# A feed-forward that makes the blocks' sums in steps: full rows of h issued with the norm

## The chip, the cores and the metric

One core of one Trainium2 chip runs the whole program as one launch. The metric is the device time of the launch in microseconds, as a median of several runs. The engines named here are PE (TensorE, matmuls), VectorE (DVE), ScalarE (ACT), and SyncE (SP), whose queue issues the loads.

## The reference, cut to what matters

The program is one inference step of a two-layer backbone on 640 tokens (512 latent, 128 context), width 1024, all in float32. Each layer is feed-forward, mixer, feed-forward. The feed-forward, and the modulation that it needs:

```python
def ffn_sub(x, g, shift, scale, gate, w_in, w_out):
    h = modulate(rms_norm(x, g), shift, scale)      # h * (1 + scale) + shift
    a, b = jnp.split(h @ w_in, 2, axis=-1)          # w_in: 1024 x 2*2816
    return x + gate * (FFN_RESIDUAL * ((jax.nn.silu(a) * b) @ w_out))

sh1, sc1, g1, sh2, sc2, g2, sh3, sc3, g3 = ada(cvec, p['w_mod'][l], p['b_mod'][l])
```

`ada` is silu(c) times a 1024 x 9216 matrix for each layer, for the latent and for the context condition.

## The kernel before

Activations lie transposed: eight tiles of 128 features by 640 tokens, split in two groups g of 320 columns. Float32 products are made from a hi and a lo half of each operand: for each weight tile ScalarE copies the hi half (L103, `whi`) and VectorE subtracts to the lo half (L104, `wlo`), and PE runs three matmuls (hi x hi, hi x lo, lo x hi; `mm3`, L132 to L135). A *unit* is one load of 128 x 1024 weights, that is one tile of 128 hidden features for a or for b: eight steps k of six matmuls for both groups, 48 matmuls. Written (2, a) here is the a-unit of hidden tile 2, counted from 0.

Of the 22 hidden tiles of each feed-forward the first `nconv` (5 in the first feed-forward, 4 in the others) are made with such units. All later ones are made by `product_set` with a scheme of Winograd's kind: seven products instead of eight on quarters of h and of the weights, 84 matmuls for an a- and a b-unit together. That scheme needs sums and differences of the four blocks h11, h12, h21, h22 of the full h (each 128 x 4 x 320, `hf`), and their hi and lo parts T1 to T4 (`Th`, `Tl`). `combine_h` makes them: first *full rows* (`h_full`, L398 on VectorE and L400 on ScalarE, one per feature tile and group), then the sums L443, L447, L448, L452 and the parts L430, L431; T4 (L436, L437) overwrites the split h after its last use. Group 1 of the full rows is made with the norm in the later feed-forwards (`apply_full`), group 0 in `combine_h`.

A later feed-forward starts with `start4`: four units, (0, a) to (1, b), are run for group 0 and then for group 1, since the norm of group 1 (`self.pend`) comes later. The first one starts with three units in `start_first`. Then `in_one` runs the units one by one, and `hidden` (L512 Silu, L516 product, L522 and L523 halves of hid) follows each pair.

Modulation: `mod_tile` loads 128 rows of w_mod (512 KB, `rawm`) and VectorE makes one sum for each condition (L157, two per tile; `sil` holds silu(c), loaded and made at L149 and L150). These tiles are fillers, given out by `filler` beside the units, product sets (`fill_set`) and output steps. They share a pool of four buffers with the weight loads (`raw`), while the split weights have five buffers (`wr`). SP issues loads in the program's order, and a load waits until its buffer is free.

In the feed-forwards the order on each engine comes from the tile scheduler, which starts from the program's order; in the mixers PE's order is written by hand. The order that was built stands further below where it matters.

Of the kernel before, what the change touches and what calls it, by code (L numbers as in the profile page):

```python
# [40 lines left out]
class Body:  # L41
# [311 lines left out]

    def start4(self, srcs, mid=None, late=None, between=None):

# [7 lines left out]
        def part(g, us):  # L363
            for u in us:
                p4[u][g] = self.bank()
            for k in range(KT):
                for u in us:
                    self.mm3([p4[u][g][:, :G]], w[u], k, [self.h(k, g)], k == 0, k == KT - 1)
                if (g, us[0], k) == (1, 1, 1) and late:
                    late()  # L370
                if (g, us[0], k) == (0, 2, 1) and self.pend:
                    self.pend()
                    self.pend = None
                    if mid:
                        self.lnexp()

        part(0, (0, 1))
# [36 lines left out]

    def combine_h(self, pool, l, s, all_groups):

        nc = self.nc
        (h11, h12), (h21, h22) = self.hf
        T = self.T = [None] * 4

        def full(r, gs):
            for k in range(4):
                for g in gs:
                    self.h_full(self.hf[r][g][:, k], 4 * r + k, g, l, s)

# [13 lines left out]
        if all_groups:  # L439
            full(0, (0, 1))  # L440
        else:
            full(0, (0,))
        nc.vector.tensor_tensor(h11, h12, h11, op=ALU.subtract)  # L443
        parts(0, h11)
        if all_groups:
            full(1, (1,))
        nc.vector.tensor_tensor(h12, h22, h12, op=ALU.subtract)  # L447
        nc.vector.tensor_tensor(h22, h22, h11, op=ALU.subtract)  # L448
        parts(1, h22)
        parts(2, h12)  # L450
        full(1, (0,))
        nc.vector.tensor_tensor(h21, h21, h22, op=ALU.subtract)  # L452
        return lambda: parts(3, h21)

# [39 lines left out]
    def ffn(self, ctx, l, j, nxt, fill=(), first=False):  # L494
# [3 lines left out]
        nconv = NCONV[2 * l + j]  # L498
        early = 8 - 4 * (nconv - 3) if first else 4
        spread = max(0, len(fill) - (32 if first else 28))  # L500
# [46 lines left out]

        def in_one(f, ab):
            w, p = self.unit(win[l, j, f, ab]), [self.bank() for _ in range(2)]
            for k in range(KT):  # L550
# [3 lines left out]
        if first:  # L554
            hid = [hidden(p3[0], p3[1])]
            hid.append(hidden(p3[2], in_one(1, 1)))
        else:
            self.h_blocks(hp)
            p4 = self.start4([win[l, j, f, ab] for f in range(2) for ab in range(2)])
            hid = [hidden(p4[0], p4[1]), hidden(p4[2], p4[3])]  # L560
        if fill:
            self.mod_load()
        if first:
            self.h_blocks(hp)
        while len(hid) < nconv:
            if len(hid) == 2:
                over = self.combine_h(Tp, l, 2 * j, first)
                self.hf = None
            pa = in_one(len(hid), 0)
            hid.append(hidden(pa, in_one(len(hid), 1)))  # L570
            if first and len(hid) > 3:
                filler(4)
        over()

# [791 lines left out]
def body(nc, tc, i, o):  # L1366
    with ExitStack() as ctx:
# [8 lines left out]
        with ExitStack() as c:  # L1376
            b.mod_begin(c)
            b.ffn(c, 0, 1, (1, 0), vf(0, range(2, 9))[52:] + vf(1, range(0, 3)))
        with ExitStack() as c:
            b.mod_begin(c)  # L1380
            b.ffn(c, 1, 0, (1, 1), vf(1, range(3, 9))[:44])
        with ExitStack() as c:
            b.mixer1(c, (1, 2))
        with ExitStack() as c:
            b.mod_begin(c)
            b.ffn(c, 1, 1, None, vf(1, range(3, 9))[44:])
        b.mm_close()
# [129 lines left out]
```

## Time and profile before

| | us |
|---|---|
| median of 3 runs | 2377.46 (2376.36 to 2379.68) |
| profiled execution | 2375.22 |
| its span | 2373.4 |
| PE busy | 2297.9 |
| VectorE busy | 1900.9 |
| ScalarE busy | 1124.8 |

The span is what the trace covers; the rest of the profiled execution lies around it. Busy times are sums over one engine's instructions. PE's is the largest by far, but matmuls are pipelined, so a busy PE need not be at full pace: the count of matmuls in a window tells its pace better.

### The profile page before, as it was taken

To read this page: it belongs to the slowest core of one execution; us is meant where nothing else is said; L and a number is where in the kernel's file an instruction comes from. 1 tells how busy PE (TensorE), PEld (TensorE's weight loads), DVE (VectorE), ACT (ScalarE), POOL (GpSimd) and SP (SyncE) were. 2 spreads that over 40 slices of the span, in tenths; PEclk is the share of its full clock that TensorE was granted. 3 is DMA by queue.
4 is the path that set the end of the run, shared out by engine and by line. 5 is a ranking of instruction groups with operands and counts; after the bars stand their busy time and mean duration, and the time that the engine had idled before them with its cause. 6 is when DMAs were issued, how large, how long until landed. Compare 5 with 4: busy or idle time off the path is not lost.

```text
span 2373.4 us, 40480 instructions
## 1 busy us (share of the span) xinstructions
PE 2297.9 (97%) x15912; PEld 2227.2 (94%) x15912; DVE 1900.9 (80%) x3779; ACT 1124.8 (47%) x2074; POOL 2.2 (0%) x10
## 2 busy tenths in 40 slices
PE   7899999999998999999999999998999999999998
PEld 4899999998888999999999999998888899999997
DVE  6998989785888978786789898969778888565665
ACT  5434343462666434334552525347756664253442
POOL 0000000000000000000000000000000000000000
PEclk9999999999999999999999999999999999999999
DMA  7354535332111434252225354432010013222221
GB/s 289 118 169 133 176 121 181 121 96 85 59 47 36 159 125 132 100 169 75 86 81 186 121 173 136 156 100 82 29 36 28 28 54 111 85 83 79 89 71 64
DMA packets 81086, 253.37 MB, mean 107 GB/s; under 512 B 9600, under 2 KB 15360, under 8 KB 80896
## 3 DMA queue, kind: packets, MB, share of 16 engines
q1 hardware_dynamic: 80896, 250.79, 32.3%
q8 instruction: 125, 2.05, 0.3%
q14 instruction: 65, 0.53, 0.1%
HBM read 247.34 MB, written 3.41 MB: 106 GB/s over the span
## 4 chain that ended last, share of the span: by engine, by line
PE 87%; DVE 9%; ACT 3%; issue 1%; DMA 1%; DVEq 0%; SPq 0%; ACTq 0%
PE mm L124 34%; PE mm L135 15%; PE mm L132 15%; PE mm L133 14%; PE tr L660 2%; PE pv L1293 2%; PE sc L1258 1%; DVE wlo L104 1%; DVE junk L157 1%; PE pv L1060 1%; ACT whi L103 0%; DVE Tl L431 0%; PE mm L810 0%; PE mm L809 0%; PE mm L808 0%
## 5 line engine op out<-in xcount | busy, mean ns | idle before, releaser
L103 ACT ACTIVATE whi<-raw 128x1024 fp32r<-128x1024 f32 (+2 forms) x419 | 406.9, 977 | 576.1 <-PE mm L133 281.1
L104 DVE TENSOR_TENSOR wlo<-raw,whi 128x1024 fp32r<-128x1024 f32 (+2 forms) x419 | 466.0, 1117 | 134.6 <-ACT whi L103 134.2
L132 PE MATMUL mm<-hid,whi 128*128 128x320 f32 x1408 | 427.1, 310 | 0.0
L133 PE MATMUL mm<-hid,whi 128*128 128x320 f32 x1408 | 425.7, 308 | 0.0
L124 PE MATMUL mm<-hhi,wlo 128*128 128x320 f32 x1136 | 351.5, 309 | 0.4 <-DVE wlo L104 0.4
L124 PE MATMUL mm<-hhi,whi 128*128 128x320 f32 x1136 | 351.3, 309 | 0.0
L124 PE MATMUL mm<-hlo,whi 128*128 128x320 f32 x1136 | 350.8, 309 | 0.0
L135 PE MATMUL mm<-hid,wlo 128*128 128x320 f32 x1408 | 346.1, 308 | 0.0
L157 DVE CUSTOM_DVE_ANT_0 junk<-rawm,sil 128x1024 bf16<-128x1024 f32 x256 | 312.0, 1219 | 16.4 <-DMA rawm<-in_wmT 14.4
L351 DVE SCALAR_TENSOR_TENSOR x<-mm,mod,x 128x192 f32<-128x192 f32 (+2 forms) x576 | 226.5, 433 | 116.8 <-PE mm L135 116.1
L132 PE MATMUL mm<-hhi,whi 128*128 128x320 f32 x896 | 280.3, 325 | 9.5 <-ACT hhi L298 6.8
L133 PE MATMUL mm<-hlo,whi 128*128 128x320 f32 x896 | 279.8, 318 | 0.5 <-DVE hlo L299 0.3
L133 PEld LDWEIGHTS mm<-hid,whi 128*128 128x128 f32 x1408 | 264.3, 188 | 0.8
L132 PEld LDWEIGHTS mm<-hid,whi 128*128 128x128 f32 x1408 | 264.3, 188 | 0.8
L135 PE MATMUL mm<-hhi,wlo 128*128 128x320 f32 x896 | 251.9, 316 | 12.9 <-DVE wlo L104 12.7
L135 PEld LDWEIGHTS mm<-hid,wlo 128*128 128x128 f32 x1408 | 241.6, 188 | 0.0
L124 PEld LDWEIGHTS mm<-hhi,wlo 128*128 128x128 f32 x1136 | 213.6, 188 | 0.8 <-DVE wlo L104 0.8
L124 PEld LDWEIGHTS mm<-hlo,whi 128*128 128x128 f32 x1136 | 213.7, 188 | 0.0
L124 PEld LDWEIGHTS mm<-hhi,whi 128*128 128x128 f32 x1136 | 213.7, 188 | 0.0
L132 PEld LDWEIGHTS mm<-hhi,whi 128*128 128x128 f32 x896 | 170.8, 193 | 19.7 <-ACT hhi L298 10.0
L135 PEld LDWEIGHTS mm<-hhi,wlo 128*128 128x128 f32 x896 | 165.1, 193 | 15.8 <-DVE wlo L104 14.9
L133 PEld LDWEIGHTS mm<-hlo,whi 128*128 128x128 f32 x896 | 173.3, 194 | 4.9 <-DVE hlo L299 2.6
(214 smaller groups left out, 4107.7 us busy)
## 6 DMA issues: line engine op xcount, KB each, us to landing
raw<-in_w_in SPq DMA_DIRECT2D x176, 512.0 KB, 3.6
rawm<-in_wmT SPq DMA_DIRECT2D x128, 512.0 KB, 3.6
raw<-in_w_out SPq DMA_DIRECT2D x64, 384.0 KB, 3.6
raw<-in_w_out SPq DMA_DIRECT2D x64, 320.0 KB, 3.0
wm<-in_wm SPq DMA_DIRECT2D x16, 512.0 KB, 10.2
raw<-in_w_ab SPq DMA_DIRECT2D x12, 512.0 KB, 4.1
raw<-in_w_c SPq DMA_DIRECT2D x10, 512.0 KB, 3.5
sil<-in_c SPq DMA_DIRECT2D x8, 512.0 KB, 5.5
```

Source lines behind the costliest of these rows:

```text
L103: a = (nc.scalar.activation(hi[:, :n], r[:, :n], AF.Copy), nc.vector.tensor_tensor(lo[:, :n], r[:, :n], hi[:, :n].bitcast(F32), op=ALU.sub ...
L104: nc.vector.tensor_tensor(lo[:, :n], r[:, :n], hi[:, :n].bitcast(F32), op=ALU.subtract))
L124: nc.tensor.matmul(out, a[:, c], b, start=start and first, stop=last, skip_group_check=True)
L132: nc.tensor.matmul(out, hi[:, c], rh, start=start, stop=False)
L133: nc.tensor.matmul(out, hi[:, c], rl, start=False, stop=False)
L135: nc.tensor.matmul(out, lo[:, c], rh, start=False, stop=stop)
L157: nc.vector.tensor_tensor_reduce(out=self.junk, in0=r, in1=self.sil[:, q], op0=ALU.mult, op1=ALU.add, scale=1.0, scalar=0.0, accum_out=sel ...
L351: nc.vector.scalar_tensor_tensor(out=x[:, c], in0=ps[:, c], scalar=self.mod[:, q, l, v, m:m + 1], in1=x[:, c], op0=ALU.mult, op1=ALU.add)
L660: self.nc.tensor.transpose(ps[:, a * P:(a + 1) * P], src[:, b * P:(b + 1) * P], self.ident)
L1060: nc.tensor.matmul(st["pv"][64 * f:64 * f + 64, ti * P:(ti + 1) * P], V[:, sl, vc[f]], st[ti, f][:, a * P:(a + 1) * P], start=a == 0, stop ...
L1258: nc.tensor.matmul(s[:, half], qs[e][:, ti * P:(ti + 1) * P], kd[kv][:, hl, half * G:half * G + G], start=hl == 0, stop=hl == 1)
L1293: nc.tensor.matmul(st["pv"][64 * f:64 * f + 64, ti * P:(ti + 1) * P], V[:, (4, 0, 1, 2, 3)[a], vc], rhs, start=a == 0, stop=a == 4)
```

## The change

The full rows of group 0 are issued in `start4`, right behind the norm of group 1, in the three later feed-forwards. `combine_h` becomes a generator: each step of it (a sum and its parts, or a set of full rows in the first feed-forward) is taken after the split of one unit of `in_one`, and what is left follows the last unit. The first feed-forward gives out its fillers singly, one per unit from hidden tile 3 on, four in all, and four in the first two product sets, where it gave out four behind each of hidden tiles 3 and 4. Eight modulation tiles move from the third feed-forward to the second.

```diff
--- before.py
+++ after.py
@@ -351,7 +351,7 @@
             nc.vector.scalar_tensor_tensor(out=x[:, c], in0=ps[:, c], scalar=self.mod[:, q, l, v, m:m + 1],
                                            in1=x[:, c], op0=ALU.mult, op1=ALU.add)
 
-    def start4(self, srcs, mid=None, late=None, between=None):
+    def start4(self, srcs, mid=None, late=None, between=None, hf=None):
 
         w = [self.unit(s) for s in srcs[:2]]
         self.hold = self.last_y
@@ -373,6 +373,9 @@
                     self.pend = None
                     if mid:
                         self.lnexp()
+                    if self.hf:
+                        for r in range(2):
+                            self.full_h(r, (0,), *hf)
 
         part(0, (0, 1))
         part(0, rest)
@@ -412,16 +415,18 @@
         self.last_hi = nc.scalar.activation(hi, t, AF.Copy)
         nc.vector.tensor_tensor(lo, t, hi.bitcast(F32), op=ALU.subtract)
 
-    def combine_h(self, pool, l, s, all_groups):
-
-        nc = self.nc
-        (h11, h12), (h21, h22) = self.hf
+    def full_h(self, r, gs, l, s):
+
+        for k in range(4):
+            for g in gs:
+                self.h_full(self.hf[r][g][:, k], 4 * r + k, g, l, s)
+
+    def combine_h(self, pool, hf, l, s, all_groups):
+
+
+        nc = self.nc
+        (h11, h12), (h21, h22) = hf
         T = self.T = [None] * 4
-
-        def full(r, gs):
-            for k in range(4):
-                for g in gs:
-                    self.h_full(self.hf[r][g][:, k], 4 * r + k, g, l, s)
 
         def parts(j, t):
             if j < 3:
@@ -437,20 +442,25 @@
                 nc.vector.tensor_tensor(lo, t[:, k], hi.bitcast(F32), op=ALU.subtract)
 
         if all_groups:
-            full(0, (0, 1))
-        else:
-            full(0, (0,))
+            self.full_h(0, (0, 1), l, s)
+            yield
         nc.vector.tensor_tensor(h11, h12, h11, op=ALU.subtract)
         parts(0, h11)
+        yield
         if all_groups:
-            full(1, (1,))
+            self.full_h(1, (1,), l, s)
+            yield
         nc.vector.tensor_tensor(h12, h22, h12, op=ALU.subtract)
         nc.vector.tensor_tensor(h22, h22, h11, op=ALU.subtract)
         parts(1, h22)
+        yield
+        if all_groups:
+            self.full_h(1, (0,), l, s)
         parts(2, h12)
-        full(1, (0,))
         nc.vector.tensor_tensor(h21, h21, h22, op=ALU.subtract)
-        return lambda: parts(3, h21)
+        yield
+        parts(3, h21)
+        yield
 
     def product_set(self, srcs):
 
@@ -496,7 +506,7 @@
         nc = self.nc
         fill = list(fill)
         nconv = NCONV[2 * l + j]
-        early = 8 - 4 * (nconv - 3) if first else 4
+        early = 4
         spread = max(0, len(fill) - (32 if first else 28))
         if first:
             with ExitStack() as cs:
@@ -545,32 +555,37 @@
             else:
                 filler((f - 6) * spread // 15 - (f - 7) * spread // 15)
 
-        def in_one(f, ab):
-            w, p = self.unit(win[l, j, f, ab]), [self.bank() for _ in range(2)]
+        def in_one(w):
+            p = [self.bank() for _ in range(2)]
             for k in range(KT):
                 self.mm3([p[g][:, :G] for g in range(2)], w, k, [self.h(k, g) for g in range(2)], k == 0, k == KT - 1)
             return p
 
         if first:
             hid = [hidden(p3[0], p3[1])]
-            hid.append(hidden(p3[2], in_one(1, 1)))
+            hid.append(hidden(p3[2], in_one(self.unit(win[l, j, 1, 1]))))
         else:
             self.h_blocks(hp)
-            p4 = self.start4([win[l, j, f, ab] for f in range(2) for ab in range(2)])
+            p4 = self.start4([win[l, j, f, ab] for f in range(2) for ab in range(2)], hf=(l, 2 * j))
             hid = [hidden(p4[0], p4[1]), hidden(p4[2], p4[3])]
         if fill:
             self.mod_load()
         if first:
             self.h_blocks(hp)
+        sums = self.combine_h(Tp, self.hf, l, 2 * j, first)
         while len(hid) < nconv:
-            if len(hid) == 2:
-                over = self.combine_h(Tp, l, 2 * j, first)
-                self.hf = None
-            pa = in_one(len(hid), 0)
-            hid.append(hidden(pa, in_one(len(hid), 1)))
-            if first and len(hid) > 3:
-                filler(4)
-        over()
+            p = []
+            for ab in range(2):
+                w = self.unit(win[l, j, len(hid), ab])
+                if (len(hid), ab) != (nconv - 1, 1):
+                    next(sums, None)
+                if first and len(hid) > 2:
+                    filler(1)
+                p.append(in_one(w))
+            hid.append(hidden(*p))
+        for _ in sums:
+            pass
+        self.hf = None
 
         def inproj(f):
             hid.append(hidden7(*self.product_set([win[l, j, f, ab] for ab in range(2)])))
@@ -1375,15 +1390,15 @@
             b.mixer0(c, (0, 2))
         with ExitStack() as c:
             b.mod_begin(c)
-            b.ffn(c, 0, 1, (1, 0), vf(0, range(2, 9))[52:] + vf(1, range(0, 3)))
+            b.ffn(c, 0, 1, (1, 0), vf(0, range(2, 9))[52:] + vf(1, range(0, 4)))
         with ExitStack() as c:
             b.mod_begin(c)
-            b.ffn(c, 1, 0, (1, 1), vf(1, range(3, 9))[:44])
+            b.ffn(c, 1, 0, (1, 1), vf(1, range(4, 9))[:36])
         with ExitStack() as c:
             b.mixer1(c, (1, 2))
         with ExitStack() as c:
             b.mod_begin(c)
-            b.ffn(c, 1, 1, None, vf(1, range(3, 9))[44:])
+            b.ffn(c, 1, 1, None, vf(1, range(4, 9))[36:])
         b.mm_close()
 
 
```

The order of instructions, on VectorE at the start of the second feed-forward. Before, from the last full rows to the lo half of unit (3, a), `wlo_8350`; `hf_7893` to `hf_7896` are h11, h12, h21, h22, and the split of (2, b) stands ahead of the first full row of group 0:

```order
L398 SCALAR_TENSOR_TENSOR hf_7895<-x_76,acol,t_7779 128x320
L443 TENSOR_TENSOR hf_7893<-hf_7894,hf_7893 128x1280
L398 SCALAR_TENSOR_TENSOR hf_7895<-x_77,acol,t_7779 128x320
L447 TENSOR_TENSOR hf_7894<-hf_7896,hf_7894 128x1280
L431 TENSOR_TENSOR Tl_8205<-hf_7893,Th_8204 128x1280
L448 TENSOR_TENSOR hf_7896<-hf_7896,hf_7893 128x1280
L431 TENSOR_TENSOR Tl_8215<-hf_7894,Th_8214 128x1280
L431 TENSOR_TENSOR Tl_8211<-hf_7896,Th_8210 128x1280
L452 TENSOR_TENSOR hf_7895<-hf_7895,hf_7896 128x1280
L516 TENSOR_TENSOR t_8339<-t_8339,mm_8289 128x320
L516 TENSOR_TENSOR t_8339<-t_8339,mm_8290 128x320
L104 TENSOR_TENSOR wlo_8350<-raw_8347,whi_8349 128x1024
```

Now, from the last full row to the lo half of unit (2, b), which is `wlo_8275` (the changed kernel's lines are some 3 to 10 higher: L447, L453, L454 are the sums, L526 and L533 belong to `hidden`):

```order
L401 SCALAR_TENSOR_TENSOR hf_7895<-x_77,acol,t_7779 128x320
L447 TENSOR_TENSOR hf_7893<-hf_7894,hf_7893 128x1280
L526 TENSOR_TENSOR t_8200<-t_8200,mm_7972 128x320
L453 TENSOR_TENSOR hf_7894<-hf_7896,hf_7894 128x1280
L436 TENSOR_TENSOR Tl_8219<-hf_7893,Th_8218 128x1280
L454 TENSOR_TENSOR hf_7896<-hf_7896,hf_7893 128x1280
L526 TENSOR_TENSOR t_8192<-t_8192,mm_8093 128x320
L526 TENSOR_TENSOR t_8200<-t_8200,mm_8095 128x320
L436 TENSOR_TENSOR Tl_8349<-hf_7894,Th_8348 128x1280
L533 TENSOR_TENSOR hid_8197<-t_8192,hid_8197 128x640
L533 TENSOR_TENSOR hid_8205<-t_8200,hid_8205 128x640
L104 TENSOR_TENSOR wlo_8275<-raw_8272,whi_8274 128x1024
```

The third part and the split of (3, a) now stand behind the split of (2, b), and the full rows of group 0 ahead of all of this, among the norm's splits.

On SyncE, whose queue issues the loads of the first feed-forward: before, from the weights of (3, a) on; `raw` are weights, `rawm` modulation tiles:

```order
L96 DMA raw_877<-in_w_in 128x1024
L96 DMA raw_933<-in_w_in 128x1024
L155 DMA rawm_997<-in_wmT 128x1024
L155 DMA rawm_1001<-in_wmT 128x1024
L155 DMA rawm_1005<-in_wmT 128x1024
L155 DMA rawm_1009<-in_wmT 128x1024
L96 DMA raw_1013<-in_w_in 128x1024
L96 DMA raw_1069<-in_w_in 128x1024
```

Now, from (3, a) on as well (`raw_842`):

```order
L96 DMA raw_842<-in_w_in 128x1024
L155 DMA rawm_864<-in_wmT 128x1024
L96 DMA raw_918<-in_w_in 128x1024
L155 DMA rawm_930<-in_wmT 128x1024
L96 DMA raw_992<-in_w_in 128x1024
L155 DMA rawm_1011<-in_wmT 128x1024
L96 DMA raw_1065<-in_w_in 128x1024
L155 DMA rawm_1071<-in_wmT 128x1024
```

Four modulation tiles in a row ahead of (4, a) have become one ahead of each unit from (3, b) on.

On VectorE in the first feed-forward, before, from the products of hidden tile 3 to the split of unit (4, b), `wlo_1072` (L157, `junk`, are the sums of the modulation tiles):

```order
L516 TENSOR_TENSOR t_989<-t_989,mm_939 128x320
L516 TENSOR_TENSOR t_989<-t_989,mm_940 128x320
L157 ISA junk,mod<-rawm_1005,sil 128x1024
L157 ISA mod 128x1
L523 TENSOR_TENSOR hid_994<-t_989,hid_994 128x640
L157 ISA junk,mod<-rawm_1009,sil 128x1024
L157 ISA mod 128x1
L104 TENSOR_TENSOR wlo_1016<-raw_1013,whi_1015 128x1024
L157 ISA junk,mod<-rawm_1009,sil 128x1024
L157 ISA mod 128x1
L104 TENSOR_TENSOR wlo_1072<-raw_1069,whi_1071 128x1024
```

Now, from the split of (3, b), `wlo_921`, on; the block sum L447 and the lo part L436 stand between the splits, and the split of (4, a) is `wlo_995`:

```order
L104 TENSOR_TENSOR wlo_921<-raw_918,whi_920 128x1024
L447 TENSOR_TENSOR hf_689<-hf_690,hf_689 128x1280
L157 ISA junk,mod<-rawm_930,sil 128x1024
L157 ISA mod 128x1
L104 TENSOR_TENSOR wlo_995<-raw_992,whi_994 128x1024
L436 TENSOR_TENSOR Tl_781<-hf_689,Th_780 128x1280
L157 ISA junk,mod<-rawm_930,sil 128x1024
L157 ISA mod 128x1
L526 TENSOR_TENSOR t_834<-t_834,mm_784 128x320
L526 TENSOR_TENSOR t_834<-t_834,mm_785 128x320
L157 ISA junk,mod<-rawm_1011,sil 128x1024
L157 ISA mod 128x1
```

The split of (4, a) stood behind seven sums of tiles and all the blocks' sums, and now stands behind three sums of tiles and the first block sum.

## Rows read from the trace of the kernel before

**Rows 1.** The page, part 1: busy time, share of the span and instructions.
```profile
PE 2297.9 (97%) x15912; PEld 2227.2 (94%) x15912; DVE 1900.9 (80%) x3779; ACT 1124.8 (47%) x2074; POOL 2.2 (0%) x10
```

**Rows 2.** Windows of 10 us, first feed-forward: length, busy (instructions), clock, DMA.
```profile
90.00:100.00 10.00, 6.66 (x41) 5.87 (x41) 9.90 (x17) 2.85 (x3) 0.00 (x0) 0.98 0.48 157
100.00:110.00 10.00, 10.00 (x60) 10.00 (x60) 9.01 (x17) 2.47 (x6) 0.00 (x0) 0.85 0.80 260
110.00:120.00 10.00, 7.14 (x39) 6.48 (x38) 9.37 (x22) 2.25 (x5) 0.00 (x0) 0.84 0.32 109
120.00:130.00 10.00, 9.49 (x64) 9.23 (x63) 8.37 (x12) 6.73 (x11) 0.00 (x0) 0.99 0.28 93
```

**Rows 3.** Windows of 20 us, feed-forwards two to four.
```profile
740.00:760.00 20.00, 20.00 (x138) 20.00 (x137) 11.60 (x23) 13.47 (x27) 0.00 (x0) 1.00 0.09 27
760.00:780.00 20.00, 16.10 (x100) 15.84 (x99) 19.52 (x23) 7.82 (x12) 0.00 (x0) 0.91 0.17 55
...
1200.00:1220.00 20.00, 16.09 (x99) 15.83 (x99) 19.71 (x23) 7.83 (x12) 0.00 (x0) 0.91 0.17 53
...
1380.00:1400.00 20.00, 20.00 (x138) 20.00 (x137) 19.63 (x39) 3.52 (x5) 0.00 (x0) 1.00 0.64 201
...
1960.00:1980.00 20.00, 16.09 (x93) 15.83 (x93) 17.55 (x22) 6.86 (x12) 0.00 (x0) 0.83 0.24 79
```

**Rows 4.** VectorE timeline, second feed-forward: start, us, instructions, idle before and releaser.
```profile
743.94 0.48 DVE L413 TENSOR_TENSOR hlo<-hf,hhi 128x320 fp32r<-128x320 f32 x1
751.49 1.23 DVE L104 TENSOR_TENSOR wlo<-raw,whi 128x1024 fp32r<-128x1024 f32 x1 [7.06 <-ACT whi L103]
752.63 0.88 DVE L516 TENSOR_TENSOR t<-t,mm 128x320 f32<-128x320 f32 x2
...
754.56 1.56 DVE L523 TENSOR_TENSOR hid<-t,hid 128x640 fp32r<-128x640 f32 x2 [0.59 <-ACT hid L522]
756.04 2.86 DVE L398 SCALAR_TENSOR_TENSOR hf<-x,acol,t 128x320 f32<-128x320 f32 x6
758.89 1.49 DVE L443 TENSOR_TENSOR hf<-hf,hf 128x1280 f32<-128x1280 f32 x1
...
764.98 2.91 DVE L431 TENSOR_TENSOR Tl<-hf,Th 128x1280 fp32r<-128x1280 f32 x2
...
770.00 1.22 DVE L104 TENSOR_TENSOR wlo<-raw,whi 128x1024 fp32r<-128x1024 f32 x1
```

**Rows 5.** ScalarE timeline, the same stretch.
```profile
751.36 0.75 ACT L512 ACTIVATE t<-mm 128x320 f32<-128x320 f32 x2
752.00 1.91 ACT L150 ACTIVATE sil<-sil 128x2048 f32<-128x2048 f32 x1
...
755.50 2.00 ACT L103 ACTIVATE whi<-raw 128x1024 fp32r<-128x1024 f32 x2
```

**Rows 6.** PE timeline, the same stretch.
```profile
771.27 0.56 PE L135 MATMUL mm<-hhi,wlo 128*128 128x320 f32 x2 [3.90 <-DVE wlo L104]
...
772.93 0.47 PE L132 MATMUL mm<-hhi,whi 128*128 128x320 f32 x1
773.20 0.47 PE L133 MATMUL mm<-hlo,whi 128*128 128x320 f32 x1
```

**Rows 7.** SyncE's DMA issues, first feed-forward.
```profile
56.90 11.62 SPq L155 DMA_DIRECT2D rawm<-in_wmT  x4
90.36 2.86 SPq L96 DMA_DIRECT2D raw<-in_w_in  x2
```

**Rows 8.** VectorE timeline, first feed-forward.
```profile
66.16 0.87 DVE L516 TENSOR_TENSOR t<-t,mm 128x320 f32<-128x320 f32 x2
...
89.10 1.22 DVE L157 CUSTOM_DVE_ANT_0 junk<-rawm,sil 128x1024 bf16<-128x1024 f32 x1
...
97.87 1.22 DVE L104 TENSOR_TENSOR wlo<-raw,whi 128x1024 fp32r<-128x1024 f32 x1
```

**Rows 9.** PE timeline, first feed-forward.
```profile
97.55 0.42 PE L132 MATMUL mm<-hhi,whi 128*128 128x320 f32 x1 [1.76 <-ACT whi L103]
```

## The prediction

> **What bounds the kernel now.** I read the page's busy table first: PE is busy 97% of the span [rows 1], so a change can only pay where PE stands still or runs slowly. The windows by stage show where that is. In undisturbed stretches PE issues 138 matmuls of 320 columns in 20 us, one per 0.145 us (first of [rows 3]). The first feed-forward falls short: between 90 and 130 us PE issues 41 + 60 + 39 + 64 = 204 [rows 2], against 276 at full pace, so 72 x 0.145 = 10.4 us are lost. The other three each have one bad stretch of 20 us, with 100, 99 and 93 matmuls instead of 138 [rows 3]: 5.5, 5.7 and 6.5 us, 17.7 in all. Together 28.1 us, all where the feed-forward begins. That is the ceiling for the edits around the blocks' sums.
>
> Then the timelines, for the cause. In the second feed-forward (the others look alike) VectorE is idle for 7.06 us until 751.49, while PE works through the last pass of the four starting units. Then VectorE works without a break: split of unit (2, b), eight rows of h, the sums and their parts, and only at 770.00 the lo half of unit (3, a) [rows 4]. PE waited 3.90 us for it, and then ran at 0.27 us per matmul, the 1.2 GHz level, for a while [rows 6]; of the 5.5 us lost, 1.6 are that.
>
> In the first feed-forward the wait has another root. SP issues four modulation tiles at 56.90 and the next unit's weights only at 90.36 [rows 7]. All share four buffers, and the first tile's second sum, which frees its buffer, stands behind the whole block of sums at 89.10. The lo half of unit (4, a) is made at 97.87 [rows 8]. PE waits 1.76 us for a hi half, among others [rows 9].
>
> **Part 1: feed-forwards two to four.** The eight full rows of group 0 move ahead of the last splits of the norm, and the sums come one step per unit, after that unit's split. No arithmetic is added or dropped. I follow VectorE in the new order (second feed-forward, durations as successive starts in rows 4). The norm's last split ended at 744.4. Into the idle 7.06 us now go eight rows (8 x 0.46 = 3.7), the first sum (1.4), a product of L516 (0.4) and the second sum (1.4): 6.9 us, to 751.3. Then a lo part 1.4, the third sum 1.4, two products 0.8, a lo part 1.4, two lo halves of hid 1.5, and the split of unit (2, b) 1.15: done at 759.0. ScalarE beside it has two Silus (0.75), the Silu of sil (1.9), two hid copies and a split (1.0) after 751.4 [rows 5], so its half is ready near 757. PE ends the starting units at 751.7 (the Silus that wait for them, rows 5), needs 48 x 0.145 = 7.0 us for unit (2, a), and asks for the lo half of (2, b) four matmuls later, at 759.3. The margin is only 0.3 us. Unit (3, a), the one that PE waits for now, is split another lo part and a split later (2.6 us), at 761.5, against a need at 766.3; the split of (3, b) follows at 764, against 773.3. So the stop goes, and (2, b) is next in line to be late.
>
> What the moved rows could hold up: five of them stand ahead of the norm's last split, 5 x 0.46 = 2.3 us, so it ends at 746.7 instead of 744.4. PE needs that piece at the last of eight steps of the pass, 12 matmuls (1.7 us) before 751.7, at 750. Cost nothing, margin 3 us. Their eight Identity instructions delay ScalarE's next Silu by a similar 3.7 us inside its idle time, and the banks that the Silu frees are wanted at 758.7.
>
> Return: 17.7 us less what is left at (2, b). I take 0.2 us each, 17.1 in all. Bounds: 17.7 if all is in time; if (2, b) comes 2 us late everywhere, 2 + 1.6 (clock as above) each remain, and the return is 6.9.
>
> **Part 2: the first feed-forward.** The same sums, and the modulation tiles of this stretch drop from eight to four, one per unit from (3, a) on; the other four go to the two product sets behind. SP's order alternates tile and weights, so a late tile holds one buffer and not all four. VectorE is done with unit (1, b)'s product at 67.0 [rows 8]. From there to the lo half of the first product set it now has: seven sums of modulation tiles at 1.2 (8.6), 24 pieces of rows (twelve 4.2, eight 2.8, four 1.8), four splits (4.6), three block sums (4.2), three lo parts (4.2), two pairs of products (1.7), three lo halves of hid (2.3) and one sum of weights (0.6): 35 us, to 102. PE, through with (1, b) at 66.1, needs six units of 7.0 and reaches the product set at 108: six us to spare, and the units before it are split as far ahead, (3, b) near 74 against a need at 87, (4, a) near 78 against 94, (4, b) near 90 against 101. So the stops of rows 2 go.
>
> What comes in their place: each of the next two product sets now carries two tiles, four sums or 4.9 us, on top of its own VectorE work, by the rates above some 8.8 us (three splits 3.5, a half split and four half sums of weights 0.6 each, four products 1.6, a lo half of hid 0.75), 13.7 us for 84 x 0.145 = 12.2 us of PE. In the new order the second set's second weights are split behind the first set's last products, one tile sum and hid, 24 us of listed work after 102: at 126 or later. PE asks for them 12.2 + 3.5 us (24 matmuls) after 108, near 124. I expect PE to wait some 2 us there, 0.4 at the first set's seed, and 1.4 us of lower clock behind it: 3.8 us. Return 10.4 - 3.8 = 6.6 us. Bounds: 10.4 (no wait), and 0 if the two sets lose all that the units gain. Behind them, each step of the output product needs 5.2 us of PE and about 4.4 us of VectorE (a split of 768 columns 0.9, three gated adds like rows of h 1.1, a tile 2.4, at the same rates), so VectorE catches up.
>
> The Trainium skill, TensorE: Matmul & The Clock Gate, Part 1, says that the lower clock is the default, that there are only the two levels, and that how busy PE has recently been decides. By it a wait as short as this, within steady work, may leave the clock alone, and the sum would be 1.4 us lower. The rows lean the other way: after waits in which 1.76 us was the longest the granted clock of 100 to 110 us was 0.85 [rows 2, 9], so the 1.4 us stay in.
>
> **Part 3: eight tiles from the third feed-forward to the second.** 8 x 2 x 1.23 = 20 us of VectorE and eight loads move. The third carries them now and its PE is not slowed where VectorE is busiest: 19.63 of 20 us busy from 1380 on, 138 matmuls [rows 3]. Cost nothing; bounds -0.5 to +2 us.
>
> **Sum.** 17.1 + 6.6 = 23.7 us. The profiled execution took 2375.2 us (span 2373.4 and 1.8 around it), 2.2 below the median shown. 2375.2 - 23.7 = 2351.5 there, 2354 as a median.
>
> **The rivals.**
> (a) Unit (2, b) late by 2 us in three feed-forwards: 10.2 us of part 1 stay, 2364. For it: a margin of 0.3 us, and ScalarE and VectorE alternate (third sum, Silus, hid), each hand-over a chance to slip. Against: I gave VectorE every instruction in sequence, and both engines have idle gaps that I did not use before 744.
> (b) The first feed-forward gains nothing, as its two product sets run at VectorE's pace (13.7 against 12.2) and the lag is not recovered: 2361. Against: the slack in the output product.
> (c) All stops go and no new one comes: 28.1, 2349.
> (d) Slower. A ring of four buffers that alternates weights and tiles passes a late tile on: a tile's second sum stands one or two units behind its first, so if it slips behind PE's next unit, each of the six following loads comes late, as now at 90.36. One such lateness cost the first feed-forward about 5 us (half of its 10.4); six would cost 30, against the 23.7 gained: 2377.5 - 23.7 + 30 = 2384; it decides from the fifth late load (25 us). Against: in the sum above, loads precede their splits by several us.
> (e) The change doesn't do what it says, the sums still standing in one piece. The order of instructions speaks against it.
>
> **Chances.** Forecast 0.62, (a) 0.13, (b) 0.10, (c) 0.06, (d) 0.04, others near no change 0.05. A measurement of this kernel cannot tell less than 0.2% (4.8 us) from no change. Faster 0.91, same 0.05, slower 0.04. The range runs from all stops gone, with 2 us of luck, to (a) with part of (b): 2347 to 2367.
>
> **What would show it.** In the new profile, PE's wait for L104's lo half at each later feed-forward (3.9 us three times) is gone or under 0.5, VectorE has no idle 7 us ahead of it, and the 20 us windows there hold over 135 matmuls. In the first, no wait for a load between 90 and 110, and one of about 2 us near 124. If PE waits there for more than 6 us, or a wait of over 1 us stands at the second unit of each feed-forward, the prediction is wrong in that part.

## The result, and the profile after

| us | before | changed |
|---|---|---|
| median | 2377.42 (2376.36 to 2379.68) | 2347.19 (2346.40 to 2348.08) |
| ratio, 95% interval | | 0.9877 (0.9866 to 0.9889) |
| profiled execution | 2375.22 | 2347.25 |
| its span | 2373.4 | 2345.5 |
| feed-forwards 1 to 4 | 399.84, 398.87, 399.96, 399.84 | 388.36, 393.17, 395.42, 393.16 |

The last row is read on ScalarE, from the table load at a feed-forward's first Silu to the table load behind the feed-forward, here of the second one in the changed kernel (1114.23 - 721.06):

```profile
721.06 1.28 ACT L522 ACT_TABLE_LOAD   x1
1114.23 1.28 ACT L247 ACT_TABLE_LOAD   x1
```

The four are 11.5, 5.7, 4.5 and 6.7 us shorter, 28.4 in all; the span is 27.9 shorter, so the rest of the program takes some 0.5 us more. The page's busy row shows the same matmuls as [rows 1] in less time:

```profile
PE 2285.8 (97%) x15912; PEld 2216.1 (94%) x15912; DVE 1902.0 (81%) x3779; ACT 1129.0 (48%) x2074; POOL 2.2 (0%) x10
```

The windows that answer [rows 3] (the second feed-forward begins 11.2 us earlier, the next two about 17 and 21; the columns are those of [rows 2] and [rows 3]: length, busy and instructions of PE, PEld, DVE, ACT, POOL, then clock, DMA share, GB/s) hold 138 or 139 matmuls where there were 93 to 100, at a granted clock of 1.00, which is 2.4 GHz:

```profile
749.00:769.00 20.00, 20.00 (x138) 20.00 (x137) 18.84 (x28) 7.13 (x12) 0.00 (x0) 1.00 0.41 134
1183.00:1203.00 20.00, 20.00 (x139) 20.00 (x138) 19.04 (x29) 7.48 (x12) 0.00 (x0) 1.00 0.40 137
1939.00:1959.00 20.00, 20.00 (x138) 20.00 (x137) 18.84 (x32) 8.83 (x14) 0.00 (x0) 1.00 0.32 106
```

VectorE's timeline in the second feed-forward, against [rows 4]: no idle 7 us, the last full rows among the norm's splits, the first sum at 735.41 and the split of unit (2, b) at 745.09.

```profile
733.56 1.94 DVE L401 SCALAR_TENSOR_TENSOR hf<-x,acol,t 128x320 f32<-128x320 f32 x4
735.41 1.49 DVE L447 TENSOR_TENSOR hf<-hf,hf 128x1280 f32<-128x1280 f32 x1
...
743.61 1.56 DVE L533 TENSOR_TENSOR hid<-t,hid 128x640 fp32r<-128x640 f32 x2
745.09 1.23 DVE L104 TENSOR_TENSOR wlo<-raw,whi 128x1024 fp32r<-128x1024 f32 x1
746.22 1.49 DVE L436 TENSOR_TENSOR Tl<-hf,Th 128x1280 fp32r<-128x1280 f32 x1
747.62 1.23 DVE L104 TENSOR_TENSOR wlo<-raw,whi 128x1024 fp32r<-128x1024 f32 x1
```

PE, against [rows 6], takes the first lo half of unit (2, b) at 748.06 and that of (3, a) at 755.10, without idle time before either (a stop would stand in brackets):

```profile
748.06 0.46 PE L135 MATMUL mm<-hhi,wlo 128*128 128x320 f32 x2
...
755.10 0.46 PE L135 MATMUL mm<-hhi,wlo 128*128 128x320 f32 x2
```

The windows of the first feed-forward, against [rows 2], are full up to 120, and the only loss in them is one wait of 0.9 us behind it (the next, 0.41 us, stands at 204.98):

```profile
90.00:100.00 10.00, 10.00 (x71) 10.00 (x70) 10.00 (x16) 4.24 (x7) 0.00 (x0) 1.00 0.32 105
100.00:110.00 10.00, 10.00 (x71) 10.00 (x70) 9.63 (x16) 5.05 (x10) 0.00 (x0) 1.00 0.01 2
110.00:120.00 10.00, 10.00 (x70) 10.00 (x70) 9.65 (x15) 4.32 (x8) 0.00 (x0) 1.00 0.63 210
120.00:130.00 10.00, 9.11 (x62) 8.84 (x61) 10.00 (x17) 5.39 (x9) 0.00 (x0) 1.00 0.43 133
```

That wait, on PE's timeline (against [rows 9]), then VectorE's and ScalarE's rows ahead of it:

```profile
125.10 0.41 PE L124 MATMUL mm<-Th,whi 128*128 128x320 f32 x1 [0.89 <-ACT mm L484]
```

```profile
99.61 1.22 DVE L104 TENSOR_TENSOR wlo<-raw,whi 128x1024 fp32r<-128x1024 f32 x1
...
121.98 0.69 DVE L476 TENSOR_TENSOR raw<-raw 128x512 f32<-128x512 f32 x1
...
124.46 2.36 DVE L104 TENSOR_TENSOR wlo<-raw,whi 128x1024 fp32r<-128x1024 f32 x2
```

```profile
122.74 1.99 ACT L103 ACTIVATE whi<-raw 128x1024 fp32r<-128x1024 f32 x2
124.63 0.42 ACT L484 ACTIVATE mm<-mm 128x320 f32<-128x320 f32 x1
```

VectorE ends the second set's weight difference (L476) at 122.67, ScalarE makes two hi halves behind it and only then the copy that the next product starts from (L484, the *seed*), done at 125.05. The lo half follows on VectorE at 125.6 and costs nothing, since PE has hi products to run first.

### The profile page after: what moved, and what is told of

Read it like the earlier page. It is cut to its first block, busy times and chain, and to the rows that moved or that the text cites. A ratio compares the mean times of both kernels' runs of the same rounds, so it can differ in the third digit from the quotient of the medians.

```text
span 2345.5 us, 40467 instructions
## 1 busy us (share of the span) xinstructions
PE 2285.8 (97%) x15912; PEld 2216.1 (94%) x15912; DVE 1902.0 (81%) x3779; ACT 1129.0 (48%) x2074; POOL 2.2 (0%) x10
## 4 chain that ended last, share of the span: by engine, by line
PE 86%; DVE 8%; ACT 2%; DMA 2%; issue 1%; SPq 0%; DVEq 0%; ACTq 0%
PE mm L124 34%; PE mm L132 15%; PE mm L133 14%; PE mm L135 14%; PE tr L675 2%; PE pv L1308 2%; DVE wlo L104 1%; PE sc L1273 1%; DVE junk L157 1%; DMA rawm<-in_wmT 1%; DMA raw<-in_w_in 1%; DVE x L351 1%; PE pv L1075 1%; ACT whi L103 1%; PE mm L823 0%
## 5 line engine op out<-in xcount | busy, mean ns | idle before, releaser
L157 DVE CUSTOM_DVE_ANT_0 junk<-rawm,sil 128x1024 bf16<-128x1024 f32 x256 | 312.4, 1220 | 19.2 <-DMA rawm<-in_wmT 14.4
L124 PEld LDWEIGHTS mm<-hlo,whi 128*128 128x128 f32 x1136 | 213.3, 188 | 0.0
L124 PEld LDWEIGHTS mm<-hhi,wlo 128*128 128x128 f32 x1136 | 213.3, 188 | 0.0
L124 PE MATMUL mm<-Th,whi 128*128 128x320 f32 x568 | 175.7, 309 | 1.9 <-ACT mm L484 1.9
L124 PE MATMUL mm<-Th,wlo 128*128 128x320 f32 x568 | 175.2, 308 | 0.0
```

The lines of the kernel that those rows point to most:

```text
L124: nc.tensor.matmul(out, a[:, c], b, start=start and first, stop=last, skip_group_check=True)
L157: nc.vector.tensor_tensor_reduce(out=self.junk, in0=r, in1=self.sil[:, q], op0=ALU.mult, op1=ALU.add, scale=1.0, scalar=0.0, accum_out=sel ...
```

## The experiments

**The two parts of the first feed-forward.** `e1` keeps the steps and gives out the tiles as before; `e2` is the kernel before with the first feed-forward's tiles given out singly. In the cuts of the edits "..." stands for lines left out.

```diff
 e1, from the changed kernel (and the later feed-forwards' lists as before)
-        early = 4
+        early = 8 - 4 * (nconv - 3) if first else 4
-                if first and len(hid) > 2:
-                    filler(1)
...
             hid.append(hidden(*p))
+            if first and len(hid) > 3:
+                filler(4)
 e2, from the kernel before
-        early = 8 - 4 * (nconv - 3) if first else 4
+        early = 4
...
-            pa = in_one(len(hid), 0)
-            hid.append(hidden(pa, in_one(len(hid), 1)))
-            if first and len(hid) > 3:
-                filler(4)
+            k = first and len(hid) > 2
+            wa = self.unit(win[l, j, len(hid), 0])
+            if k:
+                filler(1)
+            pa = in_one(wa)
... (the same for the b-unit)
```

> Steps and full rows as in the changed kernel; modulation tiles placed as before the change (four behind hidden tile 3, four behind 4, 28 and 44 tiles in the second and third feed-forward). Theory A (in the first feed-forward what counts is the sequence on VectorE; eight tile sums in a row, 9.8 us, still stand ahead of the first product set, whose weights are then split near 115 against a need at 108): the first feed-forward returns only 1 to 3 us of its 11.3, the other three return their 17, time 2358 to 2360. Rival B (the ring of load buffers was the cause: with the block's sums in steps the tiles free their buffers in time, so loads are never late): the first feed-forward returns most, time 2347 to 2351.

> The kernel before with only the tiles of the first feed-forward placed as in the changed kernel (one per unit from hidden tile 3 on, four in the first two product sets); the blocks' sums stay one piece, nothing else changes. Theory A: the split of unit (3, b) stands behind the whole block, near 89 against a need at 87, so PE waits about 3 us there and 1 to 2 us at the second product set; the first feed-forward returns 5 to 7 us, the others nothing: 2370 to 2372. Rival B (the ring alone): all 11 us return, 2366. Rival C (neither part works without the other): 0 to 2 us return, 2375 to 2377.

`e1`: 2356.76 us, ratio 0.9909 (0.9894 to 0.9924); feed-forwards 398.44, 393.16, 394.72, 393.16. `e2`: 2365.07, 0.9948 (0.9936 to 0.9961); 389.12, 398.87, 399.96, 399.81. So the first feed-forward is shortened by the placing of its tiles (10.7 of 11.5 us), hardly by the steps (1.4), and the other three by the steps alone; the two parts add up. In `e1` PE's waits are these, and VectorE's rows show the last of eight tile sums at 113.93 ahead of the split at 115.15, the time that Theory A gave:

```profile
109.50 0.42 PE L124 MATMUL mm<-hhi,whi 128*128 128x320 f32 x1 [0.58 <-ACT whi L103]
114.72 0.64 PE L124 MATMUL mm<-Th,shi 128*128 128x320 f32 x1 [4.66 <-ACT shi L113]
116.42 0.63 PE L124 MATMUL mm<-hhi,wlo 128*128 128x320 f32 x1 [0.80 <-DVE wlo L104]
```

```profile
113.33 0.68 DVE L471 TENSOR_TENSOR s<-raw 128x512 f32<-128x512 f32 x1
113.93 1.22 DVE L157 CUSTOM_DVE_ANT_0 junk<-rawm,sil 128x1024 bf16<-128x1024 f32 x1
...
115.15 1.21 DVE L104 TENSOR_TENSOR wlo<-raw,whi 128x1024 fp32r<-128x1024 f32 x1
```

At most 0.58 of these 6 us can be a late load (the first set's weights go out from 104.97 on); the rest is the queue of sums, which stands on VectorE without a gap. In `e2` SyncE still holds the weights of (4, a) until 87.73: counted from the table load at the feed-forward's first Silu that is 34.5 us, against 35.2 in the kernel before [rows 7]. In `e1` it issues the weights of (4, a) and (4, b) from 75.06 on, 15 us earlier than before (`e2`, then `e1`):

```profile
65.94 0.33 SPq L155 DMA_DIRECT2D rawm<-in_wmT  x1
87.73 0.33 SPq L96 DMA_DIRECT2D raw<-in_w_in  x1
```

```profile
75.06 4.14 SPq L96 DMA_DIRECT2D raw<-in_w_in  x2
```

So the late loads stayed in the run that returned the time, and went in the run that did not. PE's one wait ahead of the product sets in `e2` is 1.44 us at unit (3, b), half of what Theory A worked out:

```profile
87.72 0.56 PE L135 MATMUL mm<-hhi,wlo 128*128 128x320 f32 x2 [1.44 <-DVE wlo L104]
```

In `e1` Theory A's wait, its place and the return of 1.4 us held; the time is 1.2 us below its range. In `e2` Theory A's place held, but its sizes did not: the wait is half as long, at the second product set only 0.26 us are waited where it had 1 to 2, and the time is 5 us below its range. The number is that of Rival B (2366), but its reason, the ring, is not borne out: the load was as late as before.

**The two parts of the other three.** `e3` leaves the full rows out of `start4` and issues them at the head of the first step; `e4` keeps them there and takes the sums in one piece ahead of unit (2, a).

```diff
 e3, from the changed kernel
-                    if self.hf:
-                        for r in range(2):
-                            self.full_h(r, (0,), *hf)
...
+        else:
+            self.full_h(0, (0,), l, s)
+            self.full_h(1, (0,), l, s)
         nc.vector.tensor_tensor(h11, h12, h11, op=ALU.subtract)
 e4, from the changed kernel
+            if not first and len(hid) == 2:
+                for _ in range(3):
+                    next(sums)
-                if (len(hid), ab) != (nconv - 1, 1):
+                if first and (len(hid), ab) != (nconv - 1, 1):
```

> The changed kernel without the full rows behind the norm: in the three later feed-forwards the eight rows of group 0 stand at the head of the first step, behind the split of unit (2, b). VectorE's idle 7 us ahead of it stay empty. Theory A (stepping alone brings the splits in time: unit (3, a) near 762 against 766, unit (3, b) near 774.5 against 774, on the clock of the trace before): 0.5 to 1 us lost in each, time 2348 to 2351. Rival B (filling the idle time is what pays; without it the old stop comes back one unit later): 4 to 6 us lost in each, 2359 to 2364. Rival C (any wait costs the clock 1.6 us besides): 2353 to 2356.

> The changed kernel with the full rows behind the norm, but in the three later feed-forwards the sums up to the fourth block's difference in one piece ahead of unit (2, a), as before; the first feed-forward as changed. Theory A (VectorE's idle 7 us take most of the block, the split of unit (2, b) comes some 0.9 us after PE asks for it): 0.5 to 1.5 us lost in each, 2349 to 2352. Rival B (the steps are what pays): 4 to 6 us lost in each, 2359 to 2364. If both this and the run without the full rows stand within 3 us of the changed kernel, either part alone removes the stop.

`e3`: 2348.43 us, 0.9876 (0.9862 to 0.9889); 388.86, 394.22, 396.69, 394.05. `e4`: 2348.27, 0.9876 (0.9862 to 0.9889); 388.39, 393.53, 396.09, 393.65. Beside the changed kernel's, `e3` loses 1.1, 1.3 and 0.9 us, `e4` 0.4, 0.7 and 0.5, where the stop had cost 5.7: either part alone removes it (the third feed-forward, the middle figure, varies by up to 0.75 with one and the same order). In `e3` VectorE is idle as before and still has the split of (3, a) at 750.30, 5 us before 755; PE's only wait there stands at the second product set, 0.68 us at 786.20:

```profile
741.10 1.23 DVE L104 TENSOR_TENSOR wlo<-raw,whi 128x1024 fp32r<-128x1024 f32 x1 [7.05 <-ACT whi L103]
...
750.30 1.22 DVE L104 TENSOR_TENSOR wlo<-raw,whi 128x1024 fp32r<-128x1024 f32 x1
```

```profile
786.20 0.42 PE L124 MATMUL mm<-Th,whi 128*128 128x320 f32 x1 [0.68 <-ACT mm L484]
```

So in `e3` Theory A's size held nearly, but not its place: (3, b) was in time. In `e4` PE does not wait at (2, b), where Theory A had it, and the time is 0.7 us below its range. That the 0.68 us come from VectorE's lateness is argued, not shown.

**The tiles that moved to the second feed-forward.** `e5` counts them as before (28, 44, 4).

```diff
-            b.ffn(c, 0, 1, (1, 0), vf(0, range(2, 9))[52:] + vf(1, range(0, 4)))
+            b.ffn(c, 0, 1, (1, 0), vf(0, range(2, 9))[52:] + vf(1, range(0, 3)))
-            b.ffn(c, 1, 0, (1, 1), vf(1, range(4, 9))[:36])
+            b.ffn(c, 1, 0, (1, 1), vf(1, range(3, 9))[:44])
...
-            b.ffn(c, 1, 1, None, vf(1, range(4, 9))[36:])
+            b.ffn(c, 1, 1, None, vf(1, range(3, 9))[44:])
```

> The changed kernel with the later feed-forwards' modulation tiles counted as before (28, 44, 4 instead of 36, 36, 4). Theory A (the eight tiles cost nothing where they stood and nothing where they stand now): within 1 us of the changed kernel, 2346.5 to 2348; the second and the third feed-forward each within 0.7 us of their lengths in the changed kernel. Rival B (the move is part of the gain): 2 to 4 us longer, 2349 to 2351.

2346.61 us, 0.9868 (0.9853 to 0.9882): not to be told from the changed kernel. The second feed-forward is the same (393.19), the third 0.6 us shorter (394.78). All runs with 44 tiles there and the steps lie between 394.67 and 394.97, those with 36 at 395.42 and above: the move costs 0.6 us or a little more. Theory A held within its margin of 0.7 us, and the move is no part of the gain.

**The wait near 125.** The first two product sets get 0, 8 or 2 tiles (`e6`, `e7`, `e8`; `e8` with the lists of `e5`). In `e6` and `e8` the output product takes its gate before the last four or two tiles of it are made, so their results are not the reference's: they show what the placing costs and are no versions to use.

```diff
-        early = 4
-        spread = max(0, len(fill) - (32 if first else 28))
+        early = 0 if first else 4
+        spread = max(0, len(fill) - 28)
 (e7: 8 and 36, e8: 2 and 30)
```

> The changed kernel with no modulation tiles in the first two product sets of the first feed-forward; the four tiles are given out among the later product sets. Theory A (the wait of 0.89 us near 125 stands behind these tiles on VectorE, and VectorE has room later): that wait goes and no other comes, the first feed-forward 0.5 to 1 us shorter, 2346 to 2347. Rival B (VectorE has no room later, it is busy 19 of 20 us up to 280): the wait moves to a later set, 2347 to 2349.

> The changed kernel with eight modulation tiles instead of four in the first two product sets of the first feed-forward, the later sets four fewer. Theory A (each tile ahead of a split of weights costs PE its two sums, 2.45 us, as soon as there is no slack): four more sums stand ahead of the second set's second weights, PE waits 0.9 + 4.9 = 5.8 us there, and some 2 us of lower clock follow, as behind the waits of 4 to 5 us in other runs; the first feed-forward 7 to 9 us longer, 2354 to 2356. Rival B (the output product behind has slack and the loss is partly recovered): it cannot, since PE is the bound; a loss under 4 us would show that the tile sums are not what PE waits for. Rival C (four tiles clog the ring of four load buffers as in the kernel before): loads late by a further 5 us or more, 2358 to 2362.

> The changed kernel with two modulation tiles instead of four in the first two product sets of the first feed-forward, and the later feed-forwards' tiles counted as before (28, 44, 4). Theory A: the wait near 125 is 0 to 0.2 us, the second and third feed-forward as in the changed kernel within 0.7 us: 2346 to 2347, the best of the versions by under 1 us, not to be told from the changed kernel. Rival B (the moved tiles are part of the gain): 2349 to 2351.

`e6`: 2348.08 us, 0.9873 (0.9857 to 0.9890), first feed-forward 388.23. `e7`: 2355.92, 0.9907 (0.9892 to 0.9922), 397.35. `e8`: 2345.05, 0.9861 (0.9846 to 0.9875), 386.58. Without the tiles the window is full; in `e6` four matmuls are missing later (its rows are shown), in `e8` one:

```profile
120.00:130.00 10.00, 10.00 (x70) 10.00 (x69) 9.85 (x17) 4.54 (x10) 0.00 (x0) 1.00 0.75 246
...
220.00:240.00 20.00, 19.54 (x134) 19.27 (x133) 18.62 (x29) 9.58 (x17) 0.00 (x0) 1.00 0.51 164
```

With eight, 9.0 us are lost. The first wait is 3.12 us, and the clock behind it is lower:

```profile
124.83 0.41 PE L124 MATMUL mm<-Th,shi 128*128 128x320 f32 x1 [3.12 <-ACT shi L113]
```

```profile
125.00:130.00 5.00, 5.00 (x24) 4.87 (x25) 4.46 (x8) 1.99 (x4) 0.00 (x0) 0.66 0.10 30
```

Theory A's size held in `e7`, in several waits and not in one of 5.8; in `e6` Rival B was right. `e8` has no wait near 125, as its Theory A said; its time is 1 us below that range, and its interval overlaps the changed kernel's.

**Can the rest be had?** `e9` and `e10` keep all eight tiles ahead of the output product, five or six of them beside the units; `e11` and `e12` make silu(c) ahead of the first hidden tile.

```diff
 e9 (e10: early = 2, and filler(1) for every unit), with the lists of e5
-        early = 4
+        early = 3 if first else 4
-                if first and len(hid) > 2:
+                if first and (len(hid), ab) > (2, 0):
 e11 (from e5), e12 (from e9)
-        self.after(nc.scalar.activation(self.sil, self.sil, AF.Silu), self.last_silu)
+        s = nc.scalar.activation(self.sil, self.sil, AF.Silu)
+        if not early:
+            self.after(s, self.last_silu)
...
         if first:
+            self.mod_load(True)
             hid = [hidden(p3[0], p3[1])]
...
-        if fill:
+        if fill and not first:
             self.mod_load()
```

> As the run with the tiles of the later feed-forwards counted as before (28, 44, 4), with five modulation tiles beside the units of the first feed-forward (from unit (2, b) on) and three in its first two product sets, so that all eight are made before the output product needs them. Theory A (VectorE is busy without a break from 70 to 130, so a tile fewer in the sets is a tile more ahead of the first set): the 0.89 us near 125 go, and 0 to 2 us of wait come at the first set's second weights, near 112; 2345.5 to 2348. Rival B (the first set has six us to spare, as the sum ahead of it said): no wait at all between 60 and 135, 2345 to 2346.

> The same with six tiles beside the units (from unit (2, a) on) and two in the first two sets. Theory A: as above and more so; unit (4, b) is split near 102.4 against a need at 101, the first set's second weights some 2 to 3 us late, and behind waits of over 2 us some lower clock: 2347 to 2351. Rival B: no wait, 2345 to 2346.

> The changed kernel with the later feed-forwards' tiles counted as before (28, 44, 4), and with silu(c) made ahead of the first hidden tile of the first feed-forward instead of behind it, so that VectorE's idle time before 62 (2.52 us ahead of the first tile sum) can take tile sums. Theory A (VectorE's work from 60 to 125 is what sets the 0.89 us near 125): about 1.2 to 2.4 us less stands there, the wait goes, the first feed-forward 0.5 to 1 us shorter than in the run that only counts tiles as before, 2345.5 to 2346.5. Rival B: silu(c) (1.9 us on ScalarE) delays the hi half of unit (1, b) and PE waits 1 to 2 us near 60: 2347 to 2348.

> The same, with five tiles beside the units of the first feed-forward and three in its first two product sets. Theory A: the first set's second weights are split 2.4 us earlier than in the run with five and three alone (where PE waited 0.35 + 0.69 us for them and 0.51 us for a copy behind), so these waits go and none comes near 125 either: the first feed-forward 1 to 1.8 us shorter than there, 2345 to 2346.5. Rival B: as above, PE waits near 60, 2347 to 2348.

2347.98, 2347.69, 2347.97 and 2350.33 us, with intervals of the ratio within 0.9853 to 0.9896; first feed-forward 389.55, 390.04, 389.73 and 394.10. In `e11` and `e12` the first table load is that of silu(c), and it comes 0.95 us earlier against PE's matmuls than elsewhere, so their lengths compare as 388.8 and 393.2. None beats the changed kernel. `e10` has six of the eight tiles beside the units and still returns 9.8 of the 11.5 us: most of the gain is that the tiles come singly, and little that some of them move behind. Theory A held in `e9`, and in `e10` by its time, with waits of 0.2 to 0.7 us where it had 2 to 3. In `e9` the wait only moves forward, to the first set's second weights:

```profile
112.97 0.42 PE L124 MATMUL mm<-Th,whi 128*128 128x320 f32 x1 [0.35 <-ACT whi L103]
114.23 0.42 PE L124 MATMUL mm<-Th,wlo 128*128 128x320 f32 x1 [0.69 <-DVE wlo L104]
116.48 0.42 PE L124 MATMUL mm<-Th,whi 128*128 128x320 f32 x1 [0.51 <-ACT mm L484]
```

In `e11` the wait near 125 shrinks to 0.50, and some 0.8 us are lost near 60, of which the profile shows 0.18 as a wait for a hi half; in `e12` PE waits 2.65 us at the first set's second weights (115.29). Both missed their Theory A, and the trace shows its false step: the first tile sum does not come earlier but later, at 64.99 against 62.26 in `e5` and at 61.75 against 60.55 in `e9`, so VectorE's idle time ahead of it was not put to use. Why the weight difference of `e12` is then 2 us later than that of `e9`, with as many sums ahead of it, stays open.

## Why the prediction was right, and where its sizes were off

**The sum.** It gave 23.7 us; the two profiled executions differ by 27.97. Another 2.5 us of the miss of 6.8 (2354 against 2347.19) are the step from the profile to the median: 2375.2 lay 2.2 below its median, 2347.25 on it, and the rest is rounding. Which stops would go, and where a new wait would come, was right in every part; some sizes were not, nor all of the cause in part 2. And 2347.19 lies only 0.2 us inside the range, at the end that allowed for "2 us of luck": that it lies inside at all is partly luck.

**Part 1** predicted 17.1; the three feed-forwards became 16.9 us shorter, or 17.5 without the 0.6 that part 3 cost (`e5`): nearly all of the 17.7, so the 0.2 us kept back in each were not needed. The order on VectorE came as written, the split of (2, b) done at 746.3 (the sum, 11.2 us earlier by the clock of the new trace, says 747.8), and PE took it at 748.06 without a wait: a margin of 1.7 us, not 0.3. The rows among the norm's splits cost nothing. `e3` and `e4` add what the working did not say: each half would have done.

**Part 2** is the step that was mis-sized: 6.6 predicted, 11.5 measured. The split times held (99.6 for the first set's, 102 in the sum; PE there at 108.2, 108 in the sum). Three terms were wrong. First, the new wait of 3.8 us: its place was right, but it was 0.89 us, with none of the 0.4 at the first seed and none of the 1.4 of clock; 40 us hold 267 matmuls where a full stretch (740 to 780) has 275, one per 0.1465 us, so 8 x 0.1465 = 1.2 us are lost and 2.6 more returned. Second, the loss of before: ten-us windows count a matmul that crosses a border in both, and one window over the same stretch has 198, not 204:

```profile
90.00:130.00 40.00, 33.29 (x198) 31.57 (x198) 36.64 (x63) 14.31 (x23) 0.00 (x0) 0.91 0.47 155
```

```profile
90.00:130.00 40.00, 39.11 (x267) 38.84 (x266) 39.29 (x61) 19.00 (x32) 0.00 (x0) 1.00 0.35 112
```

(before, then after). 275 - 198 = 77 matmuls, 11.3 us and not 10.4: 0.9 more. Third, the stretch behind, which was not counted, holds ten matmuls more, 1.5 us:

```profile
130.00:430.00 300.00, 298.93 (x2032) 297.77 (x2031) 276.48 (x469) 116.71 (x184) 0.00 (x0) 1.00 0.48 157
```

```profile
130.00:430.00 300.00, 299.59 (x2042) 299.22 (x2041) 282.48 (x486) 119.84 (x187) 0.00 (x0) 1.00 0.50 160
```

6.6 + 2.6 + 0.9 + 1.5 = 11.6, against 11.5.

Its cause was half right. The ring of four buffers was named as the root, and PE's first waits did come from it: ScalarE stood idle for 5.50 us until the late weights of (4, a) landed. (The four tiles of [rows 7] did not go out together: the first at 56.90, the other three from 65.13 on.) But `e2` leaves the load late and still returns 10.7 us, and in `e1` the load is early and the tile sums on VectorE ahead of the splits cost 10 us all the same, at the first product set instead:

```profile
93.83 1.06 ACT L103 ACTIVATE whi<-raw 128x1024 fp32r<-128x1024 f32 x1 [5.50 <-DMA raw<-in_w_in]
```

**The clock.** After single waits of 0.89 us (changed kernel) and 1.44 us (`e2`) the granted clock stayed at 1.00. After 2.65 us (`e12`) and after 3.12 us (`e7`) it was 0.66 in a window of 5 us behind, and after 4.66 us (`e1`) 0.57 in the 10 us that hold the wait (`e12`, then `e1`):

```profile
115.00:120.00 5.00, 4.71 (x21) 4.61 (x21) 4.24 (x5) 2.69 (x5) 0.00 (x0) 0.66 0.50 163
```

```profile
110.00:120.00 10.00, 4.54 (x16) 4.08 (x16) 9.90 (x20) 1.88 (x4) 0.00 (x0) 0.57 0.38 130
```

In [rows 2] it was 0.85 after waits that [rows 9] show only the longest of; the others were 0.85 and 0.74 us, 3.35 within 5 us:

```profile
94.93 0.41 PE L132 MATMUL mm<-hhi,whi 128*128 128x320 f32 x1 [0.85 <-ACT whi L103]
...
99.14 0.56 PE L135 MATMUL mm<-hhi,wlo 128*128 128x320 f32 x2 [0.74 <-DVE wlo L104]
```

The prediction charged one wait with what three in a row had cost. The 1.4 us were not paid because the wait was 0.89 us; that a wait of the 2 us it expected would have left the clock alone is not shown, and the nearest one speaks against it: 2.21 us at 141.46 in `e7`, with 0.26 us close behind, was followed by a clock of 0.83 from 145 to 150. The Trainium skill, TensorE: Matmul & The Clock Gate, Part 1, has it that recent activity of PE decides between the two levels; the rows agree. The sum by it, 1.4 us lower, was the nearer one.

**Part 3** put the cost at nothing, within -0.5 to +2: `e5` says 0.6 us, in the third feed-forward.

**The rivals.** (a), (b), (d) and (e) did not occur; (c), all 28.1 us gone and no new wait, gave 2349 and was nearer than the forecast, at a chance of 0.06: almost that happened.

## What to carry to other kernels

Where a tuned engine waits for a split, list everything that stands ahead of it in the other engine's order: in the first feed-forward eight filler sums in a row (`e1`, 10 us lost) cost more than the whole block of sums in one piece (`e2`, 0.8 us more than the changed kernel), and giving them out singly was enough. Either filling an idle stretch or dividing a block can remove one stop; test the halves before keeping both. Count losses in one window over the whole stretch, not by adding small ones.

## What was not expected

The second and the fourth feed-forward repeat to a few hundredths of a us between the kernels that change nothing there but have the steps and the full rows of the changed kernel (393.16 to 393.19; one exception, 393.64 in the second of `e12`). The third varies by 0.75 with the same order (395.42 to 396.17), the first by 0.7 (388.36 to 389.04), and mixer 1 with its norms, from the third feed-forward's end to the fourth's start, by 2.6 (355.82 to 358.44). So the lengths of single stages tell apart what the medians, with intervals of some 3 us either way, cannot, but each stage has its own spread to be read first.
